# Encoder layer on one core: later SwiGLU tail work, weight sums two weights ahead, fewer early raw weights, whole copy of x before the low part

## Chip, cores and metric

The kernel runs on 1 core of one Trainium2 chip. The metric is the device time of one execution in microseconds; the times below are of 3 runs of the kernel before.

## The reference

One layer of an encoder over x of 256 rows and 2048 columns, all in float32. The change touches the two feed-forward networks (FFN) alone; the mixer between them and the gated embedding behind them stay as they are.

```python
def _swiglu(x, w1, w3, w2):
    return (jax.nn.silu(x @ w1) * (x @ w3)) @ w2        # w1, w3: 2048 x 5632, w2: 5632 x 2048
...
x = _layer_norm(ALPHA * x + 0.5 * _swiglu(x, ffn1_w1[i], ffn1_w3[i], ffn1_w2[i]), ln1_g[i], ln1_b[i])
mix = _hybrid_mixer(x, w_in[i], ...)
x = _layer_norm(ALPHA * x + mix, ln2_g[i], ln2_b[i])
x = _layer_norm(ALPHA * x + 0.5 * _swiglu(x, ffn2_w1[i], ffn2_w3[i], ffn2_w2[i]), ln3_g[i], ln3_b[i])
x = x + jax.nn.sigmoid(x @ w_ple_gate[i]) * (p[i] @ w_ple_proj[i])
```

## The kernel before

**Products from halves.** Each float32 operand is split into a high part rounded to fp32r and a low part, the rest. A product is hi·hi + hi·lo + lo·hi: three matmuls (L993, L994, L995). A *weight* is a tile of 256 rows and 512 columns (512 KB), loaded by SyncE into a raw page (L921). Its high part is a copy on ScalarE (L946) and its low part a subtraction on VectorE (L948) that needs the copy. A *unit* is one weight against one half of the rows (128 of the 256): two steps of 128 rows of the weight, so 6 matmuls of 128 x 512. This text numbers the units of an FFN from 0 (U0 to U499); U996 is U0 of the second FFN in the count over the whole kernel, so that its U39 is U1035.

**Chunks.** The 5632 hidden columns are 11 chunks of 512. Chunks 0, 3, 6 and 9 are computed plainly: 16 units with w1 (`gate`, Silu on ScalarE straight from PSUM into a temp), 16 units with w3 (`hidden`, VectorE multiplies, L391). Chunks 1, 2, 4, 5, 7, 8 and 10 are computed by `up7` with seven instead of eight block products: m1 and m2 (4 units each), then four rounds of m5, m7, m6, m4, m3. Some of their weights are sums of two others: made on VectorE (L296), or by a DMA that adds, issued on GpSimd (L925). `done` holds what follows a finished product: at m6 four VectorE operations (L400), at m4 and m3 one each, Silu on ScalarE (L206), two multiplications (L400, L426), and two `turn`s. A `turn` transposes 128 x 512 values on TensorE (L234, 4 instructions) into PSUM and splits them into hi (ScalarE, L228) and lo (VectorE, L229): that is the left operand of the w2 products (`down`), which add into the residual `xres` (L439).

**Order.** The program is a list of units. `main` holds the plain chunks and the downs, `weave` mixes the units of the seven `up7` in between, nearly one for one. A `down` of a chunk must come behind the chunk's turns. Work that follows a product is a generator in a heap with a due time on a planner's clock that counts TensorE time (1.3 us a unit); it is issued once that clock has passed the due time. Where a unit needs an operand that isn't issued yet, `sched.until` pulls the heap forward until it is, and the same holds for a temp (6 buffers). `DELAY["h"]` is the time from the last product to its turn. The due times place instructions in the engines' queues; each engine works its queue in order.

**Weights ahead.** `split_one` issues the two halves of one weight, up to 6 weights ahead of TensorE (`splits_due`); `make(j + 1)` issues the sum of the next weight between them. `loads` issues raw loads while fewer than 9 raw weights are held. Raw pages, halves, turned pieces and whole copies of x share 44 pages.

**x.** At the start of each FFN `transposed` turns x, 8 pieces of 128 x 512: hi, lo, and a whole float32 copy on ScalarE (L241), from which `form_turn` makes the sums of x that `up7` needs (L250 to L254, then hi and lo). In the first FFN x comes from memory (L222), in the second from the layer norm (L353 to L356).

Of the kernel before, what the change touches and what calls it, by code (L numbers as in the profile page):

```python
# [11 lines left out]
ALU = mybir.AluOpType  # L12
# [25 lines left out]


DELAY = {  # L40
    "after": 14.0, "form": 18.0, "ln_turn": 5.0, "ln_step": 1.7, "h": 3.0, "mt": 3.2,
    "sbt": 4.6, "g0": 3.0, "g1": 4.0, "g2": 12.0, "cv0": 1.0, "cv1": 3.5, "cv2": 1.3,
    "m0": 3.0, "m1": 0.6, "m2": 0.6, "m3": 4.6, "m4": 4.6, "s0": 6.6, "s1": 6.7, "s2": 5.0,
}
# [62 lines left out]
class Weight:  # L107


    def __init__(self, raw, loads, frees, make=None):  # L110
        self.raw, self.loads, self.frees, self.make = raw, loads, frees, make
        self.cols, self.uses, self.index, self.made = raw.cols, 0, None, False


# [40 lines left out]
def kernel(  # L155
# [27 lines left out]
    def drop(n=1):  # L183
        temps[0] -= n
# [46 lines left out]
    def transposed(src, act, c, t):  # L231
        ps = misc([P, 4, P])
        for k in range(4):
            nc.tensor.transpose(ps[:, k], src[:, k * P:(k + 1) * P], ident[:])  # L234
        dst = act.get(c, t)
        split_psum(dst[:, 0], dst[:, 1], ps[:])
        act.mark(c, t, 4)
        if act.forms:
            if c not in act.whole:
                act.whole[c] = big()  # L240
            nc.scalar.copy(act.whole[c][:, t * COL:(t + 1) * COL], ps.rearrange("q k s -> q (k s)"))  # L241
        if act.forms and all(act.ready(c, h) for h in range(TT)):
            sched.spawn(form_turn(act, c), DELAY["form"] + 5.0 * c)

    def form_turn(act, c):

        a = [act.whole[c][:, t * COL:(t + 1) * COL] for t in range(TT)]
        s12, s34 = temp(), temp()
        l, r = slice(0, 2 * P), slice(2 * P, 4 * P)
        nc.vector.tensor_tensor(out=s12[:, l], in0=a[1][:, r], in1=a[1][:, l], op=ALU.subtract)  # L250
        nc.vector.scalar_tensor_tensor(out=s12[:, r], in0=s12[:, l], scalar=-1.0, in1=a[0][:, l],
                                       op0=ALU.mult, op1=ALU.subtract)
        nc.vector.tensor_tensor(out=s34[:, l], in0=a[0][:, l], in1=a[1][:, l], op=ALU.subtract)
        nc.vector.tensor_tensor(out=s34[:, r], in0=a[0][:, r], in1=s12[:, r], op=ALU.add)  # L254
        for h, src in enumerate((s12, s34)):
            dst = act.forms.get(c, h)
            split_psum(dst[:, 0], dst[:, 1], src.rearrange("q (k s) -> q k s", s=P))
            drop()
            act.forms.mark(c, h, 4)
        return  # L260
        yield


    def rows_of(w, r, col0, cols):
# [16 lines left out]
    def seven(wa, wb, rows, col0, cols, act, done):  # L281

        n = rows // (4 * P)
        accs = {m: {} for m in range(1, 8)}

        def unit(m, i, tile, src, half, sub):
            return Unit(tile, half, accs[m], src, i, sub, i == 0, i == n - 1, lambda ps, t, m=m: done(m, ps))

        def plus(out, a, b):
            def make():
                nc.vector.tensor_tensor(out=out.tile[:, :, :cols], in0=a.tile[:, :, :cols], in1=b.tile[:, :, :cols],  # L296
                                        op=ALU.add)
            return make

        units = []  # L300
        for m, sub in ((1, 0), (2, 2)):
            for i in range(n):
                units.append(unit(m, i, plain(rows_of(wa, (4 * i + sub) * P, col0, cols)), act, 0, sub))
        for i in range(n):
            b11, b12, b22, b21 = (rows_of(w, (4 * i + sub) * P, col0, cols)
                                  for w, sub in ((wa, 0), (wb, 0), (wb, 2), (wa, 2)))
            t1 = Raw(b12.src, cols, b11.src)
            t3, add = (Raw(b12.src, cols, b22.src), None) if i % 2 else (b12, plus(b12, b12, b22))
            units += [
                unit(5, i, Weight(t1, [t1], []), act.forms, 0, 0),  # L310
                unit(7, i, Weight(t3, [t3, b22], [t3], add), act.forms, 1, 0),
                unit(6, i, Weight(t1, [], [], plus(t1, t1, b22)), act.forms, 0, 2),
                unit(4, i, Weight(b21, [b21], [t1, b21], plus(b21, t1, b21)), act, 1, 2),
                unit(3, i, Weight(b22, [], [b22]), act.forms, 1, 2),
            ]
        return units
# [56 lines left out]
    def ffn(w1, w3, w2, act, norm, skew=True):  # L373
# [22 lines left out]
        def up7(c):  # L396
            r, held = {}, {}

            def both(out, a, b, op):
                nc.vector.tensor_tensor(out=out, in0=a, in1=b, op=op)  # L400

            def done(m, ps):
                held[m] = ps
                if m == 1:
                    r["u"] = temp()
                    nc.scalar.copy(r["u"][:], ps)
                elif m == 2:
                    r["g0"] = temp()
                    both(r["g0"][:], ps, r["u"][:], ALU.add)
                    activate(r["g0"][:], r["g0"][:], ACT.Silu)  # L410
                elif m == 6:
                    u, v, z = r["u"], temp(), temp()
                    both(u[:], ps, u[:], ALU.add)
                    both(v[:], held[5], u[:], ALU.add)
                    both(u[:], held[7], u[:], ALU.add)
                    both(z[:], held[5], u[:], ALU.add)
                    r["v"], r["z"] = v, z
                elif m == 4:
                    u = r["u"]
                    both(u[:], ps, u[:], ALU.add)  # L420
                    activate(u[:], u[:], ACT.Silu)
                elif m == 3:
                    u, v, z = r["u"], r["v"], r["z"]
                    both(v[:], ps, v[:], ALU.subtract)
                    both(v[:], v[:], r["g0"][:], ALU.mult)
                    nc.vector.scalar_tensor_tensor(out=z[:], in0=z[:], scalar=-1.0, in1=u[:],  # L426
                                                   op0=ALU.mult, op1=ALU.mult)
                    drop(2)
                    sched.spawn(turn(v, c, 0), DELAY["h"])
                    sched.spawn(turn(z, c, 1), DELAY["h"] + 2.0)  # L430

            return seven(w1, w3, D, c * COL, COL, act, done)

        def down(c, m):
            pairs = []
            for g in range(D // COL):
                def add(ps, t, g=g):
# [8 lines left out]
        gate, hidden = zip(*(up(c) for c in (0, 3, 6, 9)))  # L446
        program.extend((skewed(gate[0][:SKEW]) if skew else flat(gate[0][:SKEW])) + flat(gate[0][SKEW:]))
        last = down(8, 2)
        main = flat(hidden[0] + down(0, 1) + gate[1] + down(1, 1) + hidden[1] + down(2, 2)
                    + gate[2] + down(4, 1) + hidden[2] + down(5, 2)  # L450
                    + gate[3] + down(7, 1) + hidden[3] + last[:8])
        program.extend(main[:8] + weave(main[8:], [u for c in (1, 2, 4, 5, 7, 8, 10) for u in up7(c)]))
# [460 lines left out]
        return [slice(0, 1), slice(1, 2)] if j == 0 else [slice(0, 2)]  # L913

    def loads(most=len(raws)):
        while pos["load"] < most and pos["raw"] < limits(pos["split"])[0]:
            j = pos["load"]
            r = raws[j]
            r.tile = page_pool.tile([P, 2, COL], F32, name="raw", tag="page")
            for ks in pieces(j):  # L920
                nc.sync.dma_start(out=r.tile[:, ks, :r.cols], in_=r.src[:, ks])  # L921
                if j == 0 and ks.start == 0:
                    load_x(0, 1)
            if r.plus is not None:
                nc.gpsimd.dma_start(out=r.tile[:, :, :r.cols], in_=r.plus, accum_op=ALU.add)  # L925
            pos["load"] += 1
            pos["raw"] += 1

    def make(j):
        if j == len(weights):  # L930
            return
        w = weights[j]
        if w.make and not w.made and all(r.tile is not None for r in w.loads):
            w.make()
            w.made = True

    def split_one():
        j = pos["split"]
        w = weights[j]
        make(j)  # L940
        assert w.made or not w.make
        r = w.raw.tile[:, :, :w.cols]
        splits[j] = [page_pool.tile([P, 2, COL], F32R, name="split", tag="page") for _ in range(2)]
        hi, lo = (h[:, :, :w.cols] for h in splits[j])
        for ks in pieces(j):
            nc.scalar.copy(hi[:, ks], r[:, ks])  # L946
            make(j + 1)
            nc.vector.tensor_tensor(out=lo[:, ks], in0=r[:, ks], in1=hi[:, ks], op=ALU.subtract)  # L948
# [82 lines left out]
```

## Time and profile before

| | us |
|---|---|
| median of 3 runs | 2285.19 (2285.01 to 2285.24) |
| the profiled execution's own time | 2284.74 |
| its span, first to last instruction | 2283.0 |
| TensorE busy | 2231.5 |
| VectorE busy | 1705.4 |
| ScalarE busy | 1177.3 |

The span is 1.74 us shorter than the execution's own time. Durations are of one execution. In the views, PE is TensorE, DVE VectorE, ACT ScalarE, POOL GpSimd, SP SyncE. A group of instructions shows, after its count, busy time in us, mean ns of one, and the idle time before it with what ended that. A timeline row shows start in us, duration in us, engine, line, operation, and in brackets the idle time before it and what it waited for. Matmuls overlap, so a row's duration is longer than the distance to the next.

### The profile page before, as it was taken

What the parts mean: (1) busy time and instruction counts of PE and PEld (TensorE: products, weight loads), DVE (VectorE), ACT (ScalarE), POOL (GpSimd) and SP (SyncE); (2) the same over time, 40 slices, a digit from 0 to 9 for tenths busy, and PEclk for the clock granted to TensorE, in tenths of its full rate; (3) what the DMA queues carried; (4) which work ended last, traced back from release to release, by engine and by line L of the source; (5) the groups of instructions that cost most, each with busy time, mean ns of one, the idle gap of its engine ahead of it and who ended that gap; (6) DMA issues with size and microseconds to landing.
All of it is one profiled execution on the core that took longest, in us unless ns stands there. A gap on an engine that the chain in (4) does not pass through costs nothing.

```text
span 2283.0 us, 27662 instructions
## 1 busy us (share of the span) xinstructions
PE 2231.5 (98%) x10107; PEld 1840.8 (81%) x10107; DVE 1705.4 (75%) x1878; ACT 1177.3 (52%) x1379; POOL 146.6 (6%) x131
## 2 busy tenths in 40 slices
PE   8899999999999999999999999989999999999999
PEld 6788788888887888888888888778878888788878
DVE  5789788888888765654555466688978888888873
ACT  6455455555554555545653354355545555555452
POOL 2000001001000000100100000200100100000000
PEclk9999999999999999999999999999999999999999
DMA  8799799999994665665566666579979999999643
GB/s 304 221 281 295 236 287 289 283 281 276 285 323 156 189 185 159 174 184 149 174 184 187 191 224 216 177 211 282 298 232 302 274 283 286 284 282 312 211 152 98
DMA packets 281353, 537.50 MB, mean 235 GB/s; under 512 B 16832, under 2 KB 25856, under 8 KB 281216
## 3 DMA queue, kind: packets, MB, share of 16 engines
q1 hardware_dynamic: 258368, 491.68, 65.4%
q0 software_dynamic: 22848, 44.05, 11.3%
q8 instruction: 79, 1.29, 0.2%
q14 instruction: 58, 0.48, 0.1%
HBM read 533.56 MB, written 2.10 MB: 235 GB/s over the span
## 4 chain that ended last, share of the span: by engine, by line
PE 89%; DVE 6%; DMA 2%; issue 2%; ACT 1%; SPq 0%; ACTq 0%; DVEq 0%
PE mm L995 29%; PE mm L993 28%; PE mm L994 28%; DMA raw<-in_ffn_w_dram 2%; DVE split L948 1%; DVE temp L400 1%; PE ms L234 1%; ACT split L946 1%; DVE xres L355 1%; DVE xres L439 1%; DVE xres L356 0%; DVE actT L229 0%; DVE xres L353 0%; DMA xres<-in_x_dram 0%; DVE stats L340 0%
## 5 line engine op out<-in xcount | busy, mean ns | idle before, releaser
L948 DVE TENSOR_TENSOR split<-raw,split 128x1024 fp32r<-128x1024 f32 (+1 forms) x989 | 1155.0, 1202 | 308.7 <-ACT split L946 296.7
L993 PE MATMUL mm<-split,actT 128*128 128x512 f32 (+2 forms) x3168 | 1239.1, 391 | 14.3 <-ACT actT L228 12.8
L995 PE MATMUL mm<-split,actT 128*128 128x512 f32 (+2 forms) x3168 | 1229.2, 388 | 15.4 <-DVE actT L229 15.4
L994 PE MATMUL mm<-split,actT 128*128 128x512 f32 (+2 forms) x3168 | 1226.7, 387 | 0.8 <-DVE split L948 0.8
L946 ACT CAST split<-raw 128x1024 fp32r<-128x1024 f32 (+1 forms) x989 | 976.6, 1035 | 429.1 <-DVE raw L296 193.0
L995 PEld LDWEIGHTS mm<-split,actT 128*128 128x128 f32 x3168 | 599.3, 189 | 143.0 <-DVE actT L229 22.3
L993 PEld LDWEIGHTS mm<-split,actT 128*128 128x128 f32 x3168 | 599.4, 189 | 134.2 <-ACT actT L228 15.7
L994 PEld LDWEIGHTS mm<-split,actT 128*128 128x128 f32 x3168 | 599.4, 189 | 118.4 <-DVE split L948 1.8
L925 POOL DMA_DIRECT2D raw<-in_ffn_w_dram x84 | 101.2, 1205 | 1137.4 <-DMA raw<-in_ffn_w_dram 356.6
L296 DVE TENSOR_TENSOR raw<-raw 128x1024 f32<-128x1024 f32 x140 | 170.3, 1216 | 0.0
L228 ACT CAST actT<-ms 128x512 fp32r<-128x512 f32 (+2 forms) x110 | 56.4, 521 | 135.2 <-PE ms L234 109.7
L439 DVE SCALAR_TENSOR_TENSOR xres<-mm,xres 128x512 f32<-128x512 f32 x128 | 87.5, 686 | 42.3 <-PE mm L995 41.9
L206 ACT ACTIVATE temp<-temp 128x512 f32<-128x512 f32 (+1 forms) x44 | 26.1, 593 | 168.3 <-DVE temp L400 146.1
L229 DVE TENSOR_TENSOR actT<-ms,actT 128x512 fp32r<-128x512 f32 (+2 forms) x110 | 65.2, 602 | 40.5 <-ACT actT L228 40.5
L400 DVE TENSOR_TENSOR temp<-mm,temp 128x512 f32<-128x512 f32 x98 | 67.4, 688 | 33.3 <-PE mm L995 31.5
L370 POOL TENSOR_SCALAR xres<-xres 128x512 f32<-128x512 f32 x16 | 25.4, 1588 | 332.9 <-DVE xres L353 300.5
L206 ACT ACTIVATE temp<-mm 128x512 f32<-128x512 f32 (+1 forms) x26 | 14.6, 565 | 61.1 <-PE mm L995 61.1
L206 ACT ACTIVATE big<-mm 128x512 f32<-128x512 f32 x20 | 12.0, 598 | 55.8 <-PE mm L995 55.8
L234 PE MATMUL ms<-ident,temp 128*128 128x128 f32 x176 | 28.8, 292 | 11.2 <-DVE temp L400 11.2
L234 PEld LDWEIGHTS ms<-ident,temp 128*128 128x128 f32 x176 | 22.9, 150 | 20.1 <-DVE temp L400 15.4
L873 DVE TENSOR_TENSOR temp<-temp,big 128x512 f32<-128x512 f32 (+1 forms) x10 | 5.8, 583 | 38.6 <-ACT temp L206 38.6
L787 DVE TENSOR_TENSOR big<-mm,big 128x512 f32<-128x512 f32 x16 | 11.1, 691 | 30.1 <-PE mm L995 30.1
(111 smaller groups left out, 481.1 us busy)
## 6 DMA issues: line engine op xcount, KB each, us to landing
raw<-in_ffn_w_dram SPq DMA_DIRECT2D x639, 512.0 KB, 5.8
raw<-in_w_in_dram SPq DMA_DIRECT2D x168, 512.0 KB, 3.8
raw<-in_ffn_w_dram POOLq DMA_DIRECT2D x84, 512.0 KB, 8.6
raw<-in_w_out_dram SPq DMA_DIRECT2D x32, 512.0 KB, 4.8
raw<-in_w_ple_gate_dram SPq DMA_DIRECT2D x24, 512.0 KB, 4.9
raw<-in_w_up_m_dram SPq DMA_DIRECT2D x16, 512.0 KB, 3.7
raw<-in_w_up_sb_dram SPq DMA_DIRECT2D x16, 512.0 KB, 4.3
raw<-in_w_ple_gate_dram SPq DMA_DIRECT2D x16, 256.0 KB, 4.3
```

The source lines that it names most:

```text
L228: nc.scalar.copy(hi, ps)
L229: nc.vector.tensor_tensor(out=lo, in0=ps, in1=hi, op=ALU.subtract)
L234: nc.tensor.transpose(ps[:, k], src[:, k * P:(k + 1) * P], ident[:])
L296: nc.vector.tensor_tensor(out=out.tile[:, :, :cols], in0=a.tile[:, :, :cols], in1=b.tile[:, :, :cols], op=ALU.add)
L400: nc.vector.tensor_tensor(out=out, in0=a, in1=b, op=op)
L439: nc.vector.scalar_tensor_tensor(out=xs, in0=ps, scalar=0.5, in1=xs, op0=ALU.mult, op1=ALU.add)
L925: nc.gpsimd.dma_start(out=r.tile[:, :, :r.cols], in_=r.plus, accum_op=ALU.add)
L946: nc.scalar.copy(hi[:, ks], r[:, ks])
L948: nc.vector.tensor_tensor(out=lo[:, ks], in0=r[:, ks], in1=hi[:, ks], op=ALU.subtract)
L993: nc.tensor.matmul(ps, hi, w[0][:, k, :u.cols], start=first, stop=False)
L994: nc.tensor.matmul(ps, hi, w[1][:, k, :u.cols], start=False, stop=False)
L995: nc.tensor.matmul(ps, lo, w[0][:, k, :u.cols], start=False, stop=last)
```

## The change

- In `main`, the gate of chunk 3 stands before the down of chunk 0 instead of behind it.
- In `up7`, the Silus after m2 and m4 are spawned 6 us later instead of being issued at once. After m3 only the subtraction is issued; the two multiplications follow 9 us later (`late`), and the turns 8 and 10 us behind these. `DELAY["h"]` goes from 3 to 8, also for the plain chunks (8 and 10 us).
- `form_turn` pauses 4 us between its sums and their halves.
- In `transposed` the whole copy is issued before the low part.
- `split_one` issues the sum of the weight after the next too, if the next one's is made or isn't needed; a sum that overwrites a raw weight is held back until the weight that used it before is split (`after`).
- At most 4 raw weights are held until TensorE has reached weight 6 of the kernel; splits are limited to 3 ahead until weight 8, not 7.

```diff
 DELAY = {
-    "after": 14.0, "form": 18.0, "ln_turn": 5.0, "ln_step": 1.7, "h": 3.0, "mt": 3.2,
+    "after": 14.0, "form": 18.0, "ln_turn": 5.0, "ln_step": 1.7, "h": 8.0, "silu": 6.0, "late": 9.0, "mt": 3.2,
...
         dst = act.get(c, t)
-        split_psum(dst[:, 0], dst[:, 1], ps[:])
-        act.mark(c, t, 4)
+        nc.scalar.copy(dst[:, 0], ps[:])
         if act.forms:
             if c not in act.whole:
                 act.whole[c] = big()
             nc.scalar.copy(act.whole[c][:, t * COL:(t + 1) * COL], ps.rearrange("q k s -> q (k s)"))
+        nc.vector.tensor_tensor(out=dst[:, 1], in0=ps[:], in1=dst[:, 0], op=ALU.subtract)
+        act.mark(c, t, 4)
...
         nc.vector.tensor_tensor(out=s34[:, r], in0=a[0][:, r], in1=s12[:, r], op=ALU.add)
+        yield 4.0
         for h, src in enumerate((s12, s34)):
...
-                unit(6, i, Weight(t1, [], [], plus(t1, t1, b22)), act.forms, 0, 2),
+                unit(6, i, Weight(t1, [], [], plus(t1, t1, b22), first), act.forms, 0, 2),
...
                 elif m == 2:
                     r["g0"] = temp()
                     both(r["g0"][:], ps, r["u"][:], ALU.add)
-                    activate(r["g0"][:], r["g0"][:], ACT.Silu)
+                    sched.spawn(silu(r["g0"]), DELAY["silu"])
...
                 elif m == 4:
-                    u = r["u"]
-                    both(u[:], ps, u[:], ALU.add)
-                    activate(u[:], u[:], ACT.Silu)
+                    both(r["u"][:], ps, r["u"][:], ALU.add)
+                    sched.spawn(silu(r["u"]), DELAY["silu"])
                 elif m == 3:
-                    u, v, z = r["u"], r["v"], r["z"]
-                    both(v[:], ps, v[:], ALU.subtract)
-                    both(v[:], v[:], r["g0"][:], ALU.mult)
...
-                    sched.spawn(turn(v, c, 0), DELAY["h"])
-                    sched.spawn(turn(z, c, 1), DELAY["h"] + 2.0)
+                    both(r["v"][:], ps, r["v"][:], ALU.subtract)
+                    sched.spawn(late(r["u"], r["v"], r["z"], r["g0"]), DELAY["late"])
+
+            def silu(x):
+                activate(x[:], x[:], ACT.Silu)
...
+            def late(u, v, z, g0):
+                both(v[:], v[:], g0[:], ALU.mult)
+                nc.vector.scalar_tensor_tensor(out=z[:], in0=z[:], scalar=-1.0, in1=u[:], op0=ALU.mult, op1=ALU.mult)
+                drop(2)
+                sched.spawn(turn(v, c, 0), DELAY["h"])
+                sched.spawn(turn(z, c, 1), DELAY["h"] + 2.0)
...
-        main = flat(hidden[0] + down(0, 1) + gate[1] + down(1, 1) + hidden[1] + down(2, 2)
+        main = flat(hidden[0] + gate[1] + down(0, 1) + down(1, 1) + hidden[1] + down(2, 2)
...
-        while pos["load"] < most and pos["raw"] < limits(pos["split"])[0]:
+        while pos["load"] < most and pos["raw"] < (4 if pos["at"] < 6 else limits(pos["split"])[0]):
...
+        if w.after is not None and w.after.index >= pos["split"]:
+            return
...
             make(j + 1)
+            if weights[min(j + 1, len(weights) - 1)].made or not weights[min(j + 1, len(weights) - 1)].make:
+                make(j + 2)
...
-        most = pos["at"] + 3 if pos["at"] < 7 else len(weights)
+        most = pos["at"] + 3 if pos["at"] < 8 else len(weights)
```

More of the change, by code (lines that the diff above doesn't have):

```diff
@@ L107, with __init__ @@
 class Weight:
-    def __init__(self, raw, loads, frees, make=None):
-        self.raw, self.loads, self.frees, self.make = raw, loads, frees, make
+    def __init__(self, raw, loads, frees, make=None, after=None):
+        self.raw, self.loads, self.frees, self.make, self.after = raw, loads, frees, make, after
         self.cols, self.uses, self.index, self.made = raw.cols, 0, None, False
@@ L259, in form_turn @@
             act.forms.mark(c, h, 4)
-        return
-        yield
     def rows_of(w, r, col0, cols):
@@ L308, in seven @@
             t3, add = (Raw(b12.src, cols, b22.src), None) if i % 2 else (b12, plus(b12, b12, b22))
+            first = Weight(t1, [t1], [])
             units += [
-                unit(5, i, Weight(t1, [t1], []), act.forms, 0, 0),
+                unit(5, i, first, act.forms, 0, 0),
                 unit(7, i, Weight(t3, [t3, b22], [t3], add), act.forms, 1, 0),
-                unit(6, i, Weight(t1, [], [], plus(t1, t1, b22)), act.forms, 0, 2),
+                unit(6, i, Weight(t1, [], [], plus(t1, t1, b22), first), act.forms, 0, 2),
                 unit(4, i, Weight(b21, [b21], [t1, b21], plus(b21, t1, b21)), act, 1, 2),
@@ L418, in done @@
                 elif m == 4:
-                    u = r["u"]
-                    both(u[:], ps, u[:], ALU.add)
-                    activate(u[:], u[:], ACT.Silu)
+                    both(r["u"][:], ps, r["u"][:], ALU.add)
+                    sched.spawn(silu(r["u"]), DELAY["silu"])
                 elif m == 3:
-                    u, v, z = r["u"], r["v"], r["z"]
-                    both(v[:], ps, v[:], ALU.subtract)
-                    both(v[:], v[:], r["g0"][:], ALU.mult)
-                    nc.vector.scalar_tensor_tensor(out=z[:], in0=z[:], scalar=-1.0, in1=u[:],
-                                                   op0=ALU.mult, op1=ALU.mult)
-                    drop(2)
-                    sched.spawn(turn(v, c, 0), DELAY["h"])
-                    sched.spawn(turn(z, c, 1), DELAY["h"] + 2.0)
+                    both(r["v"][:], ps, r["v"][:], ALU.subtract)
[3 more added lines that the diff above has]
+                return
+                yield
+            def late(u, v, z, g0):
[4 more added lines that the diff above has]
+                sched.spawn(turn(z, c, 1), DELAY["h"] + 2.0)
+                return
+                yield
             return seven(w1, w3, D, c * COL, COL, act, done)
@@ L929, in make @@
     def make(j):
-        if j == len(weights):
+        if j >= len(weights):
             return
         w = weights[j]
+        if w.after is not None and w.after.index >= pos["split"]:
+            return
         if w.make and not w.made and all(r.tile is not None for r in w.loads):
```

## The prediction

> **What bounds the kernel now.** I read the page first, then TensorE's waits, then stretches around these.
>
> ```profile
> span 2283.0 us, 27662 instructions
> PE 2231.5 (98%) x10107; PEld 1840.8 (81%) x10107; DVE 1705.4 (75%) x1878; ACT 1177.3 (52%) x1379; POOL 146.6 (6%) x131
> ```
>
> TensorE is idle for 2283.0 - 2231.5 = 51.5 us only, so a change of order can gain little more than that, plus what the clock loses behind a pause. TensorE's waits name most of the 51.5 (us, times, longest):
>
> ```profile
> PE mm L995 <- DVE actT L229: 15.4, 13, 2.7
> PE mm L993 <- ACT actT L228: 12.8, 9, 3.0
> PE ms L234 <- DVE temp L400: 11.2, 10, 1.7
> ```
>
> The first two are units that wait for the low or high part of a turned piece, the third is turns that wait for the value to be turned. To price them I need TensorE's full pace; these are two matmuls of one run without a pause, 61 steps apart:
>
> ```profile
> 59.73 0.39 PE L994 MATMUL mm<-split,actT 128*128 128x512 f32 x1
> 73.56 0.39 PE L995 MATMUL mm<-split,actT 128*128 128x512 f32 x1
> ```
>
> 13.83/61 = 0.227 us a matmul, 1.36 a unit. Now the stretches (length; busy us and count for PE, PEld, DVE, ACT, POOL; granted clock; DMA):
>
> ```profile
> 73.79:91.25 17.46, 11.51 (x34) 8.09 (x32) 11.34 (x15) 8.60 (x11) 0.00 (x0) 0.73 0.73 192
> 1508.04:1526.29 18.25, 11.65 (x33) 8.07 (x32) 12.48 (x14) 8.51 (x11) 0.00 (x0) 0.72 0.64 168
> 242.88:256.26 13.38, 10.10 (x40) 7.95 (x41) 9.48 (x11) 4.60 (x6) 0.91 (x1) 0.74 0.59 155
> 1677.51:1690.17 12.66, 9.38 (x41) 7.42 (x41) 9.48 (x11) 4.60 (x6) 0.78 (x1) 0.87 0.64 159
> 92.00:165.00 73.00, 73.00 (x327) 60.37 (x327) 61.91 (x62) 38.64 (x42) 4.78 (x4) 1.00 0.89 271
> ```
>
> Place A (rows 1 and 2) is U39 to U42 of each FFN, where down 0 follows hidden 0; B (rows 3 and 4) is U153 to U156, where down 2 follows `up7(2)`. In both the clock falls to 0.72-0.87 of full. Row 5 is ordinary woven work: TensorE never pauses, VectorE has 73.0 - 61.9 = 11.1 us to spare.
>
> **The change part by part.**
>
> *Gate 3 before down 0 (A).*
>
> ```profile
> 73.79 0.60 PE L234 MATMUL ms<-ident,temp 128*128 128x128 f32 x4
> 77.12 0.50 PE L993 MATMUL mm<-split,actT 128*128 128x512 f32 x1 [2.73 <-ACT actT L228]
> 78.50 0.79 PE L995 MATMUL mm<-split,actT 128*128 128x512 f32 x1 [0.64 <-DVE actT L229]
> 85.44 0.80 PE L993 MATMUL mm<-split,actT 128*128 128x512 f32 x1 [2.42 <-ACT actT L228]
> ```
>
> TensorE turns a piece and needs it in the next unit, behind ScalarE's and VectorE's queues, twice. A holds 4 units and 8 transposes: 24 x 0.227 + 2 x 0.42 = 6.3 us at full pace (0.42 for four transposes: 339.02 to 339.44 below). It took 17.46 and 18.25, so A costs 11.2 + 12.0. In the program list hidden 0 ends at U37 in both kernels; the first down of chunk 0 moves from U39 to U67, 30 units or 41 us behind. The new due time, 8 to 10 us, fits well inside. Term: -23.2.
>
> *Silu, multiplications, turns later (C).* Eight of the ten third waits are alike; one of them:
>
> ```profile
> 333.68 0.63 ACT L206 ACTIVATE temp<-temp 128x512 f32<-128x512 f32 x1 [6.67 <-DVE temp L400]
> 335.28 2.36 DVE L948 TENSOR_TENSOR split<-raw,split 128x1024 fp32r<-128x1024 f32 x2 [1.64 <-ACT split L946]
> 339.02 0.66 PE L234 MATMUL ms<-ident,temp 128*128 128x128 f32 x4 [0.87 <-DVE temp L400]
> 339.44 0.48 PE L993 MATMUL mm<-split,actT 128*128 128x512 f32 x1
> ```
>
> ScalarE sits 6.67 us in front of a Silu whose input VectorE hasn't made; the weight halves queued behind it come late, VectorE idles 1.64 us for them, and TensorE meets the turn 3 us after m3 with its value not there. With Silu 6, multiplications 9 and turns 17-19 us after, the value is ready. The first downs of chunks 4, 5, 7, 8 and 10 stand 26, 21, 44, 37 and 18 units behind the last m3, at least 24 us, so nobody is pushed. The multiplications and turns themselves are as many as before. Term: 11.2 less two waits of 0.50 that belong to B, -10.2.
>
> *Chunks 1 and 2 are pushed (A' and B).* Here the gap is 10 and 4 units, 13.6 and 5.4 us, less than 17. Due times give way: the turn is issued right in front of the down, behind all that the two queues hold. For chunk 1 this is new (A'): before, turns at 3 us left 7 units. These rows price it:
>
> ```profile
> L948 DVE TENSOR_TENSOR split<-raw,split 128x1024 fp32r<-128x1024 f32 (+1 forms) x989 | 1155.0, 1202 | 308.7 <-ACT split L946 296.7 <-PE mm L994 4.2 <-DMA raw<-in_w_in_dram 1.9
> L946 ACT CAST split<-raw 128x1024 fp32r<-128x1024 f32 (+1 forms) x989 | 976.6, 1035 | 429.1 <-DVE raw L296 193.0 <-PE mm L995 102.0 <-PE mm L994 91.7
> L439 DVE SCALAR_TENSOR_TENSOR xres<-mm,xres 128x512 f32<-128x512 f32 x128 | 87.5, 686 | 42.3 <-PE mm L995 41.9
> L400 DVE TENSOR_TENSOR temp<-mm,temp 128x512 f32<-128x512 f32 x98 | 67.4, 688 | 33.3 <-PE mm L995 31.5
> L229 DVE TENSOR_TENSOR actT<-ms,actT 128x512 fp32r<-128x512 f32 (+2 forms) x110 | 65.2, 602 | 40.5 <-ACT actT L228 40.5
> L228 ACT CAST actT<-ms 128x512 fp32r<-128x512 f32 (+2 forms) x110 | 56.4, 521 | 135.2 <-PE ms L234 109.7 <-PE ms L739 10.5 <-PE ms L704 7.5
> ```
>
> From the end of the last m6 (U82) to the end of U95 TensorE takes 13 x 1.36 = 17.7 us. In that order of instructions VectorE does 8 operations of the chunk (8 x 0.69), 4 adds into the residual (4 x 0.68), 11 low halves (1155.0/989 = 1.17 each) and then the piece's low part (0.59): 21.7 us. It ends 4.0 us after U95, while the matmul that needs it (L995 of U96, after 0.42 of transposes and two matmuls) could run at 0.9: 3.1 us. The second piece, two units on, waits for one high half (1.04) and its own copy (0.52) on ScalarE, less the 0.42 of transposes, about 1.0. Behind stops of 2.5-2.7 us the clock fell each time: B's second row lost (1 - 0.87) x 12.66 = 1.6 us, and I add that. Together 5.7 per FFN, +11.4. Bounds: 1 if VectorE is ahead (before, at the same m6, it had been idle 3.35 us),
>
> ```profile
> 144.91 2.87 DVE L400 TENSOR_TENSOR temp<-mm,temp 128x512 f32<-128x512 f32 x4 [3.35 <-PE mm L995]
> ```
>
> and A's own 11.2-12.0, a piece turned and needed at once; I stay near the middle because the instructions are counted.
>
> The Trainium skill, "TensorE: Matmul & The Clock Gate", section "HAM oscillation — how this bites in real kernels", asks for no idle gap of TensorE above some 3.4 us. By that rule A' would keep its clock and cost 4.1 per FFN instead of 5.7; the rows disagree, as A's longest pause is 2.73 us and its clock still fell to 0.73.
>
> B was pushed already, at 3 us:
>
> ```profile
> 232.90 2.87 DVE L400 TENSOR_TENSOR temp<-mm,temp 128x512 f32<-128x512 f32 x4 [3.02 <-PE mm L995]
> 244.26 0.50 PE L993 MATMUL mm<-split,actT 128*128 128x512 f32 x1 [0.73 <-ACT actT L228]
> 247.54 0.79 PE L995 MATMUL mm<-split,actT 128*128 128x512 f32 x1 [2.55 <-DVE actT L229]
> ```
>
> The same VectorE work from 232.90 on now lacks a wait for Silu of C's size (1.64) and holds one weight half and one low part more (1.17 + 0.59 = 1.8) ahead of the part awaited: 247.7 instead of 247.54. Term 0, bounds -3 and +3 per FFN (a stop lost, or as much clock lost again as in its first row, 0.26 x 13.38 = 3.5).
>
> *Turns of plain chunks at 8 and 10 us.* Chunks 6 and 9 are needed 11 units, 15 us, after. The second turn leaves 4 us; VectorE has two halves, a sum (L296, 1.2) and the low part in front, 4.1 us, against 2 units and two matmuls, 3.2. Up to 0.9 at four places; I take +2, bounds 0 and +3.6. Chunk 0 has 41 us, chunk 3 is inside B.
>
> *Whole copy moved; form pause; fewer early raw weights (start).*
>
> ```profile
> 26.83 0.50 PE L995 MATMUL mm<-split,actT 128*128 128x512 f32 x1 [0.64 <-DVE actT L229]
> 38.32 1.24 ACT L228 CAST actT<-temp 128x512 fp32r<-128x512 f32 x2 [2.14 <-DVE temp L251]
> 42.45 0.50 PE L993 MATMUL mm<-split,actT 128*128 128x512 f32 x1 [1.15 <-ACT split L946]
> 43.71 0.50 PE L994 MATMUL mm<-split,actT 128*128 128x512 f32 x1 [0.76 <-DVE split L948]
> 42.00:77.00 35.00, 31.18 (x130) 25.19 (x130) 31.99 (x40) 22.69 (x29) 3.77 (x3) 0.95 0.73 214
> 1458.00 0.59 ACT L241 COPY big<-ms 128x512 f32<-128x512 f32 x1 [4.59 <-DVE actT L229]
> 1461.61 0.69 DVE L229 TENSOR_TENSOR actT<-ms,actT 128x512 fp32r<-128x512 f32 x1 [1.14 <-ACT actT L228]
> ```
>
> The copy no longer holds ScalarE for VectorE's low part; the low part waits 0.59 for the copy. At two units of the first FFN this nets about -0.4 each, at the head of the second it frees the 1.14: -1.1. The halves of the forms leave the place before U18, where ScalarE lost 2.14: U18's 1.15 + 0.76 go, and with them the lower clock behind, (1 - 0.95) x 35 = 1.7 in that stretch. Start: -0.8 - 1.9 - 1.7 = -4.4. On SyncE's queue two pieces of x (0.5 MB together) pass two raw weights, at 192-271 GB/s 2-3 us; these weights are some units ahead. I take -4, bounds -5 and +2.
>
> *Sums two weights ahead.* No instruction is added; VectorE reaches 84 sums one weight earlier. What hides it is the lead of 6 weights; the cost without that is the last rival. GpSimd's adding DMAs keep their number. Term 0.
>
> Sum: -23.2 - 10.2 + 11.4 + 0 + 2 - 4 - 1.1 = -25.1. From the profiled 2284.74 that gives 2259.6; the median of the runs is 0.45 higher, so **2260**.
>
> **The rivals.**
> - *A' costs nothing worth naming* (1 per FFN, half the other delays): 10 us less, 2250. For it: VectorE's 3.35 us of idleness there. Against it: the adds of down 0 now fall into that stretch.
> - *A only moves*: A' costs A's 11.6. +11.8, 2272. For it: the same form, a turn and its user side by side. Against: 10 units in between let all but the turn be done.
> - *The delays do nothing*: VectorE is as late after 17 us as after 3, C stays, and A' is full: 2272 + 10 = 2282. Against: its spare 11.1 us per 73.
> - *Slower: VectorE is blocked by sums whose weights haven't landed.*
>
> ```profile
> L296 DVE TENSOR_TENSOR raw<-raw 128x1024 f32<-128x1024 f32 x140 | 170.3, 1216 | 0.0
> raw<-in_ffn_w_dram SPq DMA_DIRECT2D x639, 512.0 KB, 5.8
> raw<-in_ffn_w_dram POOLq DMA_DIRECT2D x84, 512.0 KB, 8.6
> ```
>
> No sum waited before (0.0). Six sums per `up7` come one weight earlier; if each waits the 8.6 - 5.8 = 2.8 us by which an adding load is slower, that is 16.8 us per `up7` of 85 us, in which VectorE has 11.1/73 x 85 = 12.9 to spare. It decides from 2.2 us per sum. Then 14 x 3.9 = 55 us on top: 2315. Against it: that zero.
>
> **How the numbers follow.** Forecast (2252 to 2267) 45%, A' cheap 17%, A moves 18%, delays useless 10%, blocked sums 10%. The range takes the first three and their bounds, 2244 to 2278; the forecast's own is 2252 to 2267. 0.2% of 2285 is 4.6 us. Faster: 45 + 17 + 18 and half of the fourth, 85%; the same 5%; slower 10%.
>
> **What would show it.** A right: no pause at U39, clock 1.00 there. C right: turns wait for L400 at most at B. A' right: 2-4 us of waiting at U96 and U98, clock below 1. Start right: U18 begins near 38. The forecast is wrong if TensorE's idle time stays near 50 us, if L296 shows idle time, or if units wait for L948.

## Result and profile after

| | before | after |
|---|---|---|
| median of 4 runs, us | 2285.1 (2284.1 to 2285.24) | 2252.14 (2250.94 to 2253.55) |
| the profiled execution's own time | 2284.74 | 2253.55 |
| its span | 2283.0 | 2251.8 |

The ratio is 0.9857, with an interval of 0.984 to 0.9874. The forecast was 2260 in a range of 2244 to 2278.

The first lines of the page of after, and the group of the sums (count, busy us, mean ns, idle time before):

```profile
span 2251.8 us, 27730 instructions
PE 2217.1 (98%) x10107; PEld 1833.9 (81%) x10107; DVE 1698.0 (75%) x1878; ACT 1191.7 (53%) x1383; POOL 149.3 (7%) x131
...
L296 DVE TENSOR_TENSOR raw<-raw 128x1024 f32<-128x1024 f32 x140 | 170.8, 1220 | 1.0
```

TensorE is idle for 2251.8 - 2217.1 = 34.7 us instead of 51.5, and its count of instructions is the same. The sums, as many as before, wait 1.0 us in all. In the changed file the code stands some lines further down: the three matmuls of a unit are L1005, L1006 and L1007, the high and low part of a turned piece L236 and L241, the whole copy L240, the weight halves L956 and L960, and the operations after a product L401. The timeline and waits views below show chosen rows.

TensorE's waits after (us in total, times, longest):

```profile
PE mm L1007 <- DVE actT L241: 10.5, 10, 2.7
PE mm L1005 <- ACT actT L236: 7.6, 8, 1.7
PE ms L234 <- DVE temp L401: 5.6, 2, 2.8
```

Turns waited ten times for their value (11.2 us); two of these waits are left, one per FFN, and they are at B. Units still wait for both parts of a turned piece, 18.1 us instead of 28.2. Where they do is seen in stretches of after (length; busy us and count of PE, PEld, DVE, ACT, POOL; granted clock; DMA):

```profile
42.00:77.00 35.00, 35.00 (x160) 29.00 (x159) 33.41 (x43) 22.51 (x28) 3.77 (x3) 1.00 0.95 278
...
66.34:74.00 7.66, 7.66 (x38) 6.34 (x37) 7.63 (x12) 4.06 (x6) 0.00 (x0) 1.00 1.05 238
145.35:158.40 13.05, 10.01 (x38) 7.04 (x37) 8.00 (x8) 7.43 (x9) 2.41 (x2) 0.87 0.85 259
229.50:244.90 15.40, 11.10 (x45) 8.00 (x44) 10.04 (x12) 5.19 (x7) 0.00 (x0) 0.89 0.60 148
1566.60:1579.60 13.00, 9.96 (x38) 7.17 (x37) 7.92 (x8) 7.52 (x9) 1.20 (x1) 0.87 0.79 240
1650.60:1666.00 15.40, 11.09 (x47) 8.27 (x46) 10.04 (x12) 5.18 (x7) 0.00 (x0) 0.89 0.60 155
```

The first row is the stretch behind U18 that ran at 0.95 of the clock before; the second is U39 and what follows, where TensorE is busy for all 7.66 us. The third and fifth rows are U96 to U100, a place where the kernel before had no pause at all: here TensorE stands still for 3.0 us and the clock falls to 0.87. The fourth and sixth are B.

To compare places I took from both traces the time between the last matmuls of two units and subtracted full pace: 0.2267 us for each matmul (13.83/61, as in the prediction) and 0.105 for each transpose (0.42/4). What is left is the loss, in us, first FFN / second FFN:

| place | units | before | after | change | forecast |
|---|---|---|---|---|---|
| start or head | U0 to U24 | 8.93 / 5.58 | 2.10 / 4.08 | -6.8, -1.5 | -4, -1.1 |
| A | U39 to U43 | 11.58 / 11.98 | 0.05 / 0.05 | -23.5 | -23.2 |
| A' | U96 to U100 | 0 / 0 | 5.85 / 5.71 | +11.6 | +11.4 |
| B | U153 to U157 | 7.03 / 6.32 | 7.32 / 7.07 | +1.0 | 0 |
| C, four places | from U217, U343, U407, U470 | 6.36 / 6.34 | 0 / 0 | -12.7 | -10.2 |
| turns of plain chunks | all the rest | 0.5 / 0.5 | 0.8 / 0.8 | +0.6 | +2 |

The column sums to -31.3; the span became 31.2 us shorter. From the last matmul of U499 to the last one before the second FFN, where the mixer stands, 710.5 us pass in both kernels.

### The profile page after: what moved, and what is told of

The parts are those of the page before. It is cut to its first block, busy times and chain, and to the rows that moved or that the text cites. A ratio compares the mean times of both kernels' runs of the same rounds, so it can differ in the third digit from the quotient of the medians.

```text
span 2251.8 us, 27730 instructions
## 1 busy us (share of the span) xinstructions
PE 2217.1 (98%) x10107; PEld 1833.9 (81%) x10107; DVE 1698.0 (75%) x1878; ACT 1191.7 (53%) x1383; POOL 149.3 (7%) x131
## 4 chain that ended last, share of the span: by engine, by line
PE 95%; DVE 3%; ACT 1%; issue 1%; DMA 1%; DVEq 0%; ACTq 0%
PE mm L1007 31%; PE mm L1005 31%; PE mm L1006 31%; PE ms L234 1%; DVE xres L356 1%; DVE actT L241 0%; DVE split L960 0%; DVE xres L354 0%; DMA raw<-in_ffn_w_dram 0%; DVE xres L357 0%; DVE stats L341 0%; ACT actT L236 0%; PE ms L724 0%; PE ms L747 0%; PE ms L675 0%
## 5 line engine op out<-in xcount | busy, mean ns | idle before, releaser
L960 DVE TENSOR_TENSOR split<-raw,split 128x1024 fp32r<-128x1024 f32 (+1 forms) x989 | 1152.9, 1204 | 286.0 <-ACT split L956 278.7
L956 ACT CAST split<-raw 128x1024 fp32r<-128x1024 f32 (+1 forms) x989 | 989.2, 1037 | 484.8 <-PE mm L1007 184.3
L1005 PE MATMUL mm<-split,actT 128*128 128x512 f32 (+2 forms) x3168 | 1235.0, 390 | 7.6 <-ACT actT L236 7.6
L1007 PE MATMUL mm<-split,actT 128*128 128x512 f32 (+2 forms) x3168 | 1225.2, 387 | 10.7 <-DVE actT L241 10.5
L1006 PE MATMUL mm<-split,actT 128*128 128x512 f32 (+2 forms) x3168 | 1222.9, 386 | 0.0
L1007 PEld LDWEIGHTS mm<-split,actT 128*128 128x128 f32 x3168 | 597.1, 188 | 137.2 <-DVE actT L241 17.4
L1005 PEld LDWEIGHTS mm<-split,actT 128*128 128x128 f32 x3168 | 597.4, 189 | 126.0 <-ACT actT L236 9.7
L1006 PEld LDWEIGHTS mm<-split,actT 128*128 128x128 f32 x3168 | 597.6, 189 | 116.4 <-DVE split L960 0.6
L236 ACT CAST actT<-ms 128x512 fp32r<-128x512 f32 x84 | 48.9, 589 | 147.9 <-PE ms L234 147.9
L241 DVE TENSOR_TENSOR actT<-ms,actT 128x512 fp32r<-128x512 f32 x84 | 57.0, 687 | 39.3 <-ACT actT L236 26.8
L401 DVE TENSOR_TENSOR temp<-mm,temp 128x512 f32<-128x512 f32 x98 | 67.4, 688 | 21.0 <-PE mm L1007 19.5
L407 ACT COPY temp<-mm 128x512 f32<-128x512 f32 x14 | 8.2, 588 | 60.4 <-PE mm L1007 60.4
```

The source lines that it names most:

```text
L236: nc.scalar.copy(dst[:, 0], ps[:])
L241: nc.vector.tensor_tensor(out=dst[:, 1], in0=ps[:], in1=dst[:, 0], op=ALU.subtract)
L1005: nc.tensor.matmul(ps, hi, w[0][:, k, :u.cols], start=first, stop=False)
L1006: nc.tensor.matmul(ps, hi, w[1][:, k, :u.cols], start=False, stop=False)
L1007: nc.tensor.matmul(ps, lo, w[0][:, k, :u.cols], start=False, stop=last)
```

## Experiments

Theory: the whole gain is the sum of the table. The moved gate is worth 23.5; the delays take away C (12.7) and give it back as A' (11.6), because due times that don't fit in front of a down are cut short and the turn is issued at the last moment; the start brings the rest. Rivals: the delays bring a net gain of their own, and the move alone wins less (the A-only-moves idea); and, for the start, any one of three edits may be its cause. All ratios are to the kernel before on the same chip (medians 2282.31 to 2283.48).

**The move alone.** The kernel before with one edit:

```diff
-        main = flat(hidden[0] + down(0, 1) + gate[1] + down(1, 1) + hidden[1] + down(2, 2)
+        main = flat(hidden[0] + gate[1] + down(0, 1) + down(1, 1) + hidden[1] + down(2, 2)
```

> The kernel before with one edit: the gate of chunk 3 stands before the down of chunk 0. My theory (place A alone goes; C, B and the start stay as they were; nothing is pushed at U96, since turns come 3 us after m3): 2285 less 23.5 = 2261.5 us, TensorE's waits for turns (L234 on DVE temp) still 10 times and some 11 us, U96 without a pause. Rival (A only moves to the first down of chunk 1 because down 0 and down 1 together load VectorE, whatever the delays): 2273 us, with some 5.8 us lost at U96 to U100 of each FFN.

Measured: 2261.38 (2259.14 to 2262.96), ratio 0.9903 (0.9886 to 0.992). A loses 0.14 / 0.11, U96 nothing. TensorE's waits in it:

```profile
PE mm L995 <- DVE actT L229: 13.1, 9, 2.7
PE ms L234 <- DVE temp L400: 11.7, 12, 1.7
PE mm L993 <- ACT actT L228: 2.6, 5, 0.7
```

The waits for L228, 12.8 us before with a longest of 3.0, are down to 2.6, and the turns' waits for L400 are all still there: twelve instead of ten, as each FFN has a small new one at U89, where chunk 1 is turned and some 0.3 us are lost. About 22 us come from where one block of units stands, and behind U24 this small stop is the only new one.

**All delays taken out of after.**

```diff
-    ... "h": 8.0, "silu": 6.0, "late": 9.0, ...
+    ... "h": 3.0, "silu": 0.0, "late": 0.0, ...
```

> The changed kernel with the old due times (turn 3, Silu and multiplications 0 us after); move, start and sums stay. Theory: the delays gave 12.7 us (C) and took 11.6 (A', the pushed turns of chunk 1), so without them the time hardly moves: 2252 + 12.7 - 11.6 = 2253 us, with eight waits for turns back and U96 without a pause. Rival (A' comes from VectorE's load, not from the push): A' stays and C comes back, 2265 us. Rival (the delays carry the gain): about 2265 us or more as well, but then with no loss at U96.

Measured: 2253.31 (2253.23 to 2253.57), ratio 0.9869 (0.9854 to 0.9884). The four C places lose 1.18, 2.02, 1.79 and 1.41 again in each FFN, A' nothing, and the waits show it:

```profile
PE mm L1007 <- DVE actT L241: 12.9, 9, 2.7
PE ms L234 <- DVE temp L401: 11.7, 12, 1.7
PE mm L1005 <- ACT actT L236: 1.5, 2, 0.7
```

Twelve waits of turns instead of two (eight at C, two at B, and the two at U89 that the move alone has too), and two waits for L236 instead of eight. With its delays after takes 2252.14, without them 2253.31; the two intervals overlap. The three delays move the stops of eight places to two others, and for the time no gain of theirs can be told from the noise.

**Shorter delays.** If A' comes only from due times that don't fit into the 13.6 us in front of chunk 1's down, shorter ones should keep C's gain without it.

```diff
-    ... "h": 8.0, "silu": 6.0, "late": 9.0, ...
+    ... "h": 4.0, "silu": 2.0, "late": 4.0, ...
```

> The changed kernel with shorter delays: Silu 2, multiplications 4, turns 4 and 6 us behind these (8 and 10 after m3, less than the 13.6 us that chunk 1 has). Theory: C stays away, A' goes, B stays pushed (7 us per FFN): 2252 - 11.5 = 2240.5 us, pauses left in the FFNs only at U153 to U156 and at the heads. Rival (VectorE's backlog is longer than the shorter delay): C comes back in part, 2241 to 2252 us, with waits for turns on DVE temp at U217, U343, U407 or U470.

Measured: 2242.2 (2239.88 to 2242.59), ratio 0.9818 (0.9804 to 0.9833). C and A' lose nothing, B 7.03 / 7.89. Its waits, and the two stretches around A' and B:

```profile
PE mm L1007 <- DVE actT L241: 7.9, 7, 2.7
PE ms L234 <- DVE temp L401: 5.6, 2, 2.8
...
PE mm L1005 <- ACT actT L236: 2.8, 4, 0.7
```

```profile
144.00:158.00 14.00, 14.00 (x66) 11.56 (x65) 13.19 (x14) 9.47 (x11) 2.41 (x2) 1.00 1.01 307
222.00:245.00 23.00, 18.70 (x81) 14.53 (x80) 14.57 (x17) 9.59 (x13) 1.20 (x1) 0.93 0.67 180
```

At 144 to 158 us TensorE never stops: the turns of chunk 1 were issued at their own due time, and all of C's gain is kept. What is left is B, where 5.4 us in front of the down are too few for any of these delays.

**The same with the down of chunk 2 behind gate 6.** With the units of `up7` woven in, the down then starts 33 units behind chunk 2's last product instead of 4, and 45 us lie in between in this trace.

```diff
-        main = flat(hidden[0] + gate[1] + down(0, 1) + down(1, 1) + hidden[1] + down(2, 2)
-                    + gate[2] + down(4, 1) + hidden[2] + down(5, 2)
+        main = flat(hidden[0] + gate[1] + down(0, 1) + down(1, 1) + hidden[1] + gate[2]
+                    + down(2, 2) + down(4, 1) + hidden[2] + down(5, 2)
```

> The same shorter delays, and the down of chunks 2 and 3 stands behind the gate of chunk 6 instead of before it, so that no turn is pushed anywhere in the FFNs. Theory (B is the push of chunk 2 alone): B's 7.3 and 7.1 us go too, 2240.5 - 14.4 = 2226 us, and between U24 and U495 TensorE has no pause over half a microsecond. Rival (B's loss is VectorE's backlog behind m6, and moves with the next down): about 2240 us.

Measured: 2227.74 (2226.03 to 2228.7), ratio 0.9756 (0.9742 to 0.9771): the fastest of all, 24 us below after (23 by the two ratios). The stretch around the former B, and what TensorE still waits for:

```profile
222.00:245.00 23.00, 23.00 (x111) 19.16 (x110) 21.30 (x23) 13.59 (x16) 3.61 (x3) 1.00 0.89 244
```

```profile
PE mm L1007 <- DVE actT L241: 8.1, 7, 2.7
PE ms L234 <- DVE xres L357: 3.1, 2, 2.6
...
PE mm L1006 <- DVE split L960: 0.4, 1, 0.4
```

In the same 23 us TensorE passes 111 matmuls and transposes instead of 81. No turn waits for a product's value any more; what is left stands at the heads of the FFNs and behind the norms.

**The long delays, with the downs further back.** This asks whether the length of the delays or the push was the cost: after as it is, and only the order changed.

```diff
-        main = flat(hidden[0] + gate[1] + down(0, 1) + down(1, 1) + hidden[1] + down(2, 2)
-                    + gate[2] + down(4, 1) + hidden[2] + down(5, 2)
+        main = flat(hidden[0] + gate[1] + down(0, 1) + hidden[1] + down(1, 1)
+                    + gate[2] + down(2, 2) + down(4, 1) + hidden[2] + down(5, 2)
```

> The changed kernel with its own long delays, and the downs of chunks 1 and 2 moved later (down 1 behind hidden 3, down 2 behind the gate of chunk 6), so that no turn is pushed. Theory (A' and B are the push, not the length of the delay): 2252 - 11.6 - 14.4 = 2226 us, the same as short delays with the later down 2 (2227.7), no loss at the first downs of chunks 1 and 2. Rival (temps held longer, or two downs back to back, make VectorE late): 2230 us or more, with waits elsewhere between U24 and U495.

Measured: 2228.67 (2226.99 to 2229.03), ratio 0.9767 (0.9751 to 0.9783). A' and B lose 0, and so do the new places of these downs (U125 and U182, at most 0.12 us a unit), with Silu still at 6, multiplications at 9 and turns 8 and 10 us behind. So the delays cost nothing where they fit; the push does.

**The early limits undone.** After with 9 raw weights from the start and splits free from weight 7:

```diff
-        while pos["load"] < most and pos["raw"] < (4 if pos["at"] < 6 else limits(pos["split"])[0]):
+        while pos["load"] < most and pos["raw"] < limits(pos["split"])[0]:
...
-        most = pos["at"] + 3 if pos["at"] < 8 else len(weights)
+        most = pos["at"] + 3 if pos["at"] < 7 else len(weights)
```

> The changed kernel with the early limits of before: 9 raw weights held from the start, splits free from weight 7 of the kernel on. The first FFN's U0 to U24 lost 8.9 us before and 2.1 after. Theory (the gain there is the forms' pause and the whole copy; the limits add little): 2252 to 2254 us, U0 to U24 loses 2 to 4 us. Rival (the order of x against raw weights, or the Silu in front of weight 9's halves, made U18's stop): 2256 to 2257 us, a stop of about 2 us at U18 and a clock window below 1 behind it.

Measured: 2251.64 (2250.22 to 2252.94), ratio 0.9861 (0.9845 to 0.9878); U0 to U24 lose 2.12. The limits do nothing here.

**The pause in `form_turn` undone.**

```diff
-        yield 4.0
...
+        return
+        yield
```

> The changed kernel without the pause of 4 us in form_turn. Theory (ScalarE's 2.14 us in front of the forms was one half of U18's stop): 2253 to 2256 us, ScalarE idle before the forms' copies again, U18 late by 1 to 2 us with some clock lost. Rival (the later split limit alone cured U18): 2252 us.

Measured: 2252.49 (2250.23 to 2254.89), ratio 0.9867 (0.9852 to 0.9882). A stop of 0.79 us is back between U16 and U20, and U0 to U24 lose 2.86. It can't be told from after by its time. Its A' is of interest further down.

**The whole copy behind the low part again.**

```diff
-        nc.scalar.copy(dst[:, 0], ps[:])
+        split_psum(dst[:, 0], dst[:, 1], ps[:])
+        act.mark(c, t, 4)
...
-        nc.vector.tensor_tensor(out=dst[:, 1], in0=ps[:], in1=dst[:, 0], op=ALU.subtract)
-        act.mark(c, t, 4)
```

> The changed kernel with the whole copy of x behind the low part again. Theory: ScalarE waits again for each low part, 16 times 1.6 us; the head of the second FFN loses its 1.1 to 1.5 us again and U9 and U13 of the first 0.4 each: 2254 us, U996 to U1020 back from 4.1 to 5.6 us lost. Rival (nothing on TensorE's path): 2252 us.

Measured: 2257.21 (2255.5 to 2258.05), ratio 0.9886 (0.9872 to 0.9901): 5 us slower than after, more than the 2 us expected. The loss is 4.30 at the start, 1.05 of the increase in U1 to U7, and 5.88 at the head of the second FFN (2.10 and 4.08 in after). So its trace places 4.0 of the 5, and the 1.05 go with a late start of the full clock that is left open below. ScalarE's waits in it:

```profile
ACT big L241 <- DVE actT L229: 26.0, 16, 4.6
```

All 16 copies wait for VectorE's low part of the same piece, and whatever ScalarE has behind them, weight halves and the next piece, waits with them.

**The early limits and the pause both undone.** The theory was that either hides the other.

```diff
-        while pos["load"] < most and pos["raw"] < (4 if pos["at"] < 6 else limits(pos["split"])[0]):
+        while pos["load"] < most and pos["raw"] < limits(pos["split"])[0]:
...
-        most = pos["at"] + 3 if pos["at"] < 8 else len(weights)
+        most = pos["at"] + 3 if pos["at"] < 7 else len(weights)
...
-        yield 4.0
```

> The changed kernel with both start edits that did little alone undone together: early limits of before (9 raw weights, splits free from weight 7) and no pause in form_turn. Theory (each cures U18's stop alone, so that undoing one shows nothing): U18's stop of about 2 us is back, with a clock drop behind it or not; U0 to U24 loses 4.5 to 6.5 us instead of 2.1, 2254 to 2257 us. Rival (neither matters, the whole copy alone made the start): U0 to U24 at 2 to 3 us, 2252 us.

Measured: 2252.76 (2252.47 to 2254.63), ratio 0.9874 (0.9859 to 0.9889). That is a miss: U16 to U20 lose 0.79, exactly as with the pause alone undone. U0 to U24 lose 3.88 in all, and the other 1.0 us by which that is more than with the pause alone undone lie in U1 to U7, where the clock was still low. At U18 the limits are worth nothing with or without the pause, and in the time neither run can be told from after.

**Sums one weight ahead again.**

```diff
-            if weights[min(j + 1, len(weights) - 1)].made or not weights[min(j + 1, len(weights) - 1)].make:
-                make(j + 2)
```

> The changed kernel with weight sums one weight ahead as before. Theory: 2252 us, nothing on TensorE moves by more than 1 us; ScalarE waits for sums (L956 on DVE raw) come back to about 190 us from what the changed kernel shows, off TensorE's path. Rival (the sums ahead keep VectorE's lead and with it A' and B small): 2255 us or more, with the losses at U96 and U153 larger by 1 us each or more.

Measured: 2250.5 (2249.76 to 2250.73), ratio 0.9857 (0.9843 to 0.9872). ScalarE's wait for the sums, first in after, then with the edit:

```profile
ACT split L956 <- DVE raw L296: 106.9, 65, 5.1
```

```profile
ACT split L956 <- DVE raw L296: 214.9, 114, 5.3
```

Two weights ahead halves this wait, by 108 us, and buys nothing: TensorE has its halves up to 6 weights early and loses at the same places in both.

## Why the prediction was right

**A, -23.2, measured -23.5.** No pause at U39, clock 1.00 there, and the move alone shows it by itself. The step was length of the stretch less work at full pace, and both were in the rows.

**A', +11.4, measured +11.6**, by the route that was forecast. TensorE, VectorE and ScalarE around U96 in after:

```profile
145.12 0.60 PE L234 MATMUL ms<-ident,temp 128*128 128x128 f32 x4
147.39 0.50 PE L1005 MATMUL mm<-split,actT 128*128 128x512 f32 x1 [1.67 <-ACT actT L236]
148.77 0.50 PE L1007 MATMUL mm<-split,actT 128*128 128x512 f32 x1 [0.64 <-DVE actT L241]
154.12 0.50 PE L1005 MATMUL mm<-split,actT 128*128 128x512 f32 x1 [0.73 <-ACT actT L236]
```

```profile
144.48 0.69 DVE L447 SCALAR_TENSOR_TENSOR xres<-mm,xres 128x512 f32<-128x512 f32 x1
145.08 1.22 DVE L960 TENSOR_TENSOR split<-raw,split 128x1024 fp32r<-128x1024 f32 x1
146.89 1.23 DVE L960 TENSOR_TENSOR split<-raw,split 128x1024 fp32r<-128x1024 f32 x1 [0.59 <-ACT split L956]
148.03 0.68 DVE L241 TENSOR_TENSOR actT<-ms,actT 128x512 fp32r<-128x512 f32 x1
```

```profile
145.32 0.59 ACT L407 COPY temp<-mm 128x512 f32<-128x512 f32 x1 [3.85 <-PE mm L1007]
145.81 1.05 ACT L956 CAST split<-raw 128x1024 fp32r<-128x1024 f32 x1
146.75 0.59 ACT L236 CAST actT<-ms 128x512 fp32r<-128x512 f32 x1
```

U95 ends where the transposes begin, at 145.12. The low part ends at 148.03 + 0.68 = 148.71, 3.6 us later; the forecast was 4.0. Two low halves stand in front of it, the second with a wait of 0.59 for a high half, and ScalarE's high part has a copy and that half in front of it. The second piece waits 0.73 (forecast 1.0), and the clock adds (1 - 0.87) x 13.05 = 1.7 (1.6). With the pause in `form_turn` undone the clock stays full here, and A' costs 4.22, against 4.1 in the forecast without its clock. That the clock falls here in after, as the forecast assumed, is luck as well: of these two kernels it falls in one.

How close 3.6 and 4.0 are is partly luck. These rows show where the count starts, TensorE and then VectorE:

```profile
126.08 0.39 PE L1005 MATMUL mm<-split,actT 128*128 128x512 f32 x1
```

```profile
126.73 2.86 DVE L401 TENSOR_TENSOR temp<-mm,temp 128x512 f32<-128x512 f32 x4
```

By the list of units the last m6 is U81 and not U82. It ends where U82 begins, at 126.08, and from there to the end of U95 TensorE takes 14 units, 19.0 us instead of 17.7. VectorE, with just the instructions that were counted, ends 22.6 us after that moment instead of 21.7: a low half was still under way (0.65) and VectorE idled 0.38 and 0.59 us, while its instructions followed each other 0.7 us closer than their durations add up to. With the right unit the forecast would have said 2.7. Counting the queue's work in the order of instructions gave the right kind and place of a wait that no row of before showed, and its size to about 1 us.

The time alone would have misled here: 2252.1 lies next to 2250, the time given for "A' costs nothing". A' cost what was forecast, and what lies between 2260 and 2252 is in other terms.

**C, -10.2, measured -12.7: under-sized.** The mechanism is as forecast. Around U217 in after, ScalarE and then VectorE:

```profile
321.06 0.64 ACT L206 ACTIVATE temp<-temp 128x512 f32<-128x512 f32 x1 [2.59 <-DVE temp L401]
```

```profile
323.21 0.68 DVE L401 TENSOR_TENSOR temp<-mm,temp 128x512 f32<-128x512 f32 x1
323.81 5.75 DVE L960 TENSOR_TENSOR split<-raw,split 128x1024 fp32r<-128x1024 f32 x5
329.48 0.68 DVE L401 TENSOR_TENSOR temp<-temp 128x512 f32<-128x512 f32 x1
```

ScalarE sits 2.59 us in front of this Silu instead of 6.67, five low halves go between the subtraction and the multiplication, and no turn of these chunks waits. What failed is the pricing: the term took the idle time that the waits show. Each of the eight costs about 0.3 us more than its row shows, (12.7 - 10.2)/8. A was counted from the length of its stretch; counted in that way, C would have come out right.

**Start, -4, measured -6.8: under-sized.** U18 begins at 38.09, as forecast. Of the 6.8 us, 4.0 lie in U16 to U20 and their clock (forecast 1.9 + 1.7), 1.1 at the two units that wait for the low part (forecast 0.8), and 1.6 in U1 to U7, which the forecast had not: there the full clock began at 9.9 us instead of 13.5. That moment goes with no one edit: U1 to U7 lose 1.79 in before, 1.17 to 1.23 in the move alone, with the copy undone and with limits and pause undone (full clock from 11.6 to 12.6 us on), and 0.15 to 0.29 in the other kernels (from 7.4 to 9.9). So I leave the 1.6 open. Which edit does the rest is partly settled. Between U16 and U20 the loss is 2.47 with the copy and the pause both of before (the move alone), 0.79 with the pause undone, 0 with the copy undone: the pause is enough alone, and the copy by itself takes away two thirds. The early limits have no part in these. The head of the second FFN is the copy's (-1.5, forecast -1.1).

**B, 0, measured +1.0**, within its bounds. TensorE there in after:

```profile
232.74 0.66 PE L234 MATMUL ms<-ident,temp 128*128 128x128 f32 x4 [2.80 <-DVE temp L401]
234.06 0.50 PE L1005 MATMUL mm<-split,actT 128*128 128x512 f32 x1 [0.67 <-ACT actT L236]
240.54 0.50 PE L1005 MATMUL mm<-split,actT 128*128 128x512 f32 x1 [0.72 <-ACT actT L236]
```

Now the first turn waits 2.80 us for its multiplication, which the term had not; before it waited 0.50. The clock gives most of it back in the first FFN: (1 - 0.89) x 15.40 = 1.7 us lost instead of (1 - 0.74) x 13.38 = 3.5. So B stays near 0 by this balance and not for the reason that the forecast gave, and that is luck.

**Turns of plain chunks, +2, measured at most +0.6**: the second turns, with 4 us of time, were in front of their downs after all. **Sums two ahead, 0**, and no sum is blocked (1.0 us of idleness): the slower rival never began.

The sum was off by 31.3 - 25.1 = 6.2 us: C by 2.5, start and head by 3.2, the hidden turns by 1.4, and B by 1.0 the other way. That is the distance of the profiled execution, 2253.55, to the 2259.6 forecast for it; the median lies another 1.4 lower. Of the rivals, the two that denied A's or C's gain fall by the kernels that leave one of them out, and the cheap A' by its rows. What the prediction did not draw from its own terms is that the delays were an exchange, -12.7 against +11.6, and that the same delays, cut to half or with the downs further back, leave some 10 or 24 us more.

## What to carry to other kernels

Before lengthening a delay in a just-in-time order, find the consumers that come sooner than the new due time: there the step is issued last, behind all that the in-order queues hold, and a loss of 4 to 6 us per pair of turns can take the place of many small ones. Shorten the delay to the smallest gap or move the consumer, and check the exchange by leaving the delay out, since a change with several edits can hide one that brings nothing. Price a stop by the length of its stretch less the work at full pace, not by the idle time in its row.

## What was unexpected of the hardware

The same stops cost differently from one execution to the next. With the pause in `form_turn` undone, TensorE stops at U96 for 1.67, 0.64 and 0.73 us, as in after; but the clock stays full. The stretch of 14 us, first in after, then in that kernel:

```profile
144.00:158.00 14.00, 10.96 (x42) 7.83 (x41) 9.15 (x10) 7.06 (x9) 2.39 (x2) 0.88 0.87 263
```

```profile
144.00:158.00 14.00, 10.96 (x49) 8.08 (x49) 9.89 (x11) 7.55 (x9) 2.41 (x2) 1.00 0.98 281
```

TensorE is busy 10.96 us in both and passes 42 against 49 instructions. In after (1 - 0.88) x 14 = 1.7 us are lost to the clock, and A' costs 5.85 / 5.71; in the other kernel it costs 4.22 / 4.22. With sums one ahead it is 5.67 in the first FFN and 4.21 in the second. 1.7 us lost at half clock is a stretch of 3.4 us, and so long, or twice that, are all the half-clock stretches around stops in these traces. Whether one falls on a stop is not settled by the length of the stop.

The traces say more. In each of the twelve, the half-clock stretches begin at whole multiples of 3.413 us after the moment at which the full clock began. I cut all traces into such pieces and compared TensorE's busy share, as the profile models it, in each piece of full clock with the clock of the next one. Below 45% busy the next piece ran at half clock (48 of 48 pieces), above 55% it never did (0 of 7713), and in between it did in 8 of 29. So what counts is how much of a stop falls into one piece. The two pieces that decide here both lie in between, 1.81 and 1.74 us of 3.41 or 53% and 51%, first in after, then with the pause undone; why only the first lost its clock stays open:

```profile
146.44:149.85 3.41, 1.81 (x7) 1.19 (x8) 2.96 (x3) 1.85 (x3) 0.00 (x0) 1.00 1.05 404
```

```profile
143.96:147.37 3.41, 1.74 (x11) 1.26 (x10) 2.82 (x4) 2.20 (x4) 0.00 (x0) 1.00 1.07 332
```

The Trainium skill, "TensorE: Matmul & The Clock Gate", section "What's actually happening", describes an activity window of 3413 ns that runs freely; these stretches agree with it. What the Trainium skill asks for on the same page, section "HAM oscillation — how this bites in real kernels", no idle gap above some 3.4 us, does not protect here: stops of 1.67 and 0.64 us in a row were enough in after.

Two places that each cost 1.6 us more or not are also about the spread of after's runs, 2250.94 to 2253.55; that this is its cause was not shown, as each kernel has one trace.
